# A two-layer backbone on one core: weight sums from a column of ones in the second layer's value matmul, a matmul of its own for the values' low parts, and work moved between VectorE, GpSimd and ScalarE

## Chip, cores and metric

One of the cores of a Trainium2 chip runs the whole program. The metric is the device time of one execution in microseconds; before, the median of 3 runs is 1360.35 us.

## What is computed

Two layers over 1024 latent tokens (width 1024, 16 heads of 64) and 256 context tokens, then an RMS norm. The first layer is grouped-query attention over all tokens. The second, where most of the change lies, is attention in a neighbourhood of 8 x 16 grid cells plus all context tokens, with a learned bias:

```python
px = hx @ w_in                     # q, k, v, z: 4 x 1024 columns
...
s_nb = jnp.einsum('bqhd,bqkhd->bhqk', qr, kw).astype(jnp.float32) * ATTN_SCALE + bias
s_cx = jnp.einsum('bqhd,bshd->bhqs', qr, kc).astype(jnp.float32) * ATTN_SCALE
p = jax.nn.softmax(jnp.concatenate([s_nb, s_cx], axis=-1), axis=-1)
return (einsum(p[..., :n_nb], vw) + einsum(p[..., n_nb:], vc))
...
yx = (o * jax.nn.silu(z)) @ w_out
```

## The kernel before

Everything is float32 in value, but the matmuls take float16: each operand is split into a high part and a low part (what is left after rounding), and a product takes three matmuls, high by high, high by low, low by high.

Between the layers, `ln_pair` (L692) normalizes the token rows in pairs of tiles, forms the sums and differences that the block products below need (L704 to L707, halves of 512 columns of the two tiles), splits them (L689 on ScalarE, L690 on VectorE) and sends them through transposing DMAs (L701, L712) into `hx`. Four such pairs (t = 0, 2, 4, 6) stand among the last output products of the first layer (`a_out`, L1332). TensorE's first product of the second layer, `pwq0a`, reads what the last pair leaves.

The second layer goes by pairs of heads, u = 0 to 7. For each u:

- `b_load` (L1418) loads a float32 block of the input weights, `st`, forms four sums of its blocks on GpSimd into `tt` (L1429 to L1432), and splits both into float16 (L1434 on ScalarE, L1435 on VectorE). Two kinds and four row blocks make 8 loads a pair of heads, 64 in all. `BLK` (L1438) says which slot of the weights each of the seven block products takes.
- `b_qk` and `b_vz` (L1481, L1534) make queries, keys, values and gates by `winograd` (L1440), a scheme of seven block products instead of eight, whose sums VectorE forms from PSUM (L1457 to L1478). `put` (L1490) writes queries: the high part by ScalarE (L1499), the low part by VectorE (L1500), and a second copy of the high part into the other half of the partitions (L1501). `put_v` (L1538) writes the values' high and low parts side by side, 128 columns per head, into `v1_`.
- `b_att` (L1581) takes for each head i and each of 8 query tiles t the near key tiles (two or three) and the two context tiles. Scores come from two matmuls (L1593, L1594), bias and maximum from VectorE (L1613, L1620 to L1623), and ScalarE computes the exponentials four times: into the float16 high part `bph` (L1631, L1632), and in float32 in place (L1633, L1634) with an accumulator output that gives the sum of the weights. `p_split` (L1122) takes the low part: every fourth call (`BEV`) is one operation on VectorE (L1127), the others are two halves on GpSimd (L1130). One transposing DMA (L1637) turns both parts, and four tiles later (`BLAG`) the value matmuls follow: the transposed weights are the stationary operand, loaded anew for each matmul. The high part meets all 128 columns of the values (L1642), the low part the high 64 (L1644). `fin` (L1650) adds the two halves of the result (ScalarE's copy L1657, VectorE's L1658), and multiplies by the reciprocal of the sums (L1653 to L1655, L1659) and by the gate (L1660). It runs 32 times.

The first layer's values already have the layout that the change brings: 64 high columns, a column of ones (scaled), 64 low columns, three matmuls a key tile in `pv_mm` (L1132), and `o_evict` (L1111) at the end.

The program is written in the order that `timeline` gives to the generators. A planner in the kernel then sets each engine's order anew: it lists the instructions, schedules them with its own table of costs, and five times again with due times taken from the last schedule, keeping the shortest. So a change of one operation moves others on all engines. All DMAs of the second layer stand in SyncE's queue.

## Time and profile before

| | |
|---|---|
| median of 3 runs | 1360.35 us (1357.03 to 1361.37) |
| profiled execution | 1362.21 us, its span 1360.3 us |
| mean granted TensorE clock | 0.991 |
| TensorE, VectorE, ScalarE, GpSimd busy | 1309.5, 1129.6, 976.2, 909.9 us |

The span divides into the first layer (to about 700 us), its last output products with the normalization for the second (to about 775 us), the first pair's projections (to about 850 us), attention of one pair beside projections of the next (850 to 1250 us), and the last output product with the rest. A row of a listing gives line, engine, operation, out<-in, shapes and count, then the busy time and the mean ns of one, then the idle time of the engine ahead of it and what ended that. A row of the timeline starts with start and length in us. PEld is TensorE's weight load, which overlaps its matmuls.

### The profile page before, as it was taken

Reading aid. Unit: us, or ns where it says so; the run is one execution under the profiler, and the core shown is the slowest. Engines: PE = TensorE matmul, PEld = TensorE weight load, DVE = VectorE, ACT = ScalarE, POOL = GpSimd, SP = SyncE. Lnnn points to the kernel's source line nnn. Section 1 sums busy time; section 2 is a strip of 40 time slices with the busy share of each in tenths; the row PEclk is TensorE's granted clock in tenths of the full one; section 3 lists DMA queues with packets and bytes.
Section 4 is the critical chain, followed back from the end, with each engine's and each line's share of the span. In section 5 each row is a group of like instructions: output and inputs, shape, how many; then the busy total and the mean of one; then the engine's idle time right before and its main releaser. Section 6 shows DMA issues by size and latency. Waiting matters only on the chain.

```text
span 1360.3 us, 37879 instructions
## 1 busy us (share of the span) xinstructions
PE 1309.5 (96%) x14492; PEld 923.2 (68%) x14492; DVE 1129.6 (83%) x2603; ACT 976.2 (72%) x2325; POOL 909.9 (67%) x1251
## 2 busy tenths in 40 slices
PE   8999999999999999999999899999999999999994
PEld 4467777777777777776654357868677686876551
DVE  5898687978898787769448898899999999999668
ACT  4654889888888777788733355897978889787443
POOL 2323778777777767788775566586676778755565
PEclk9999999999999999999999999999999999999997
DMA  9634566787874222245237953587677768679953
GB/s 368 186 114 114 118 125 144 153 153 146 141 142 104 66 77 60 57 118 139 79 109 175 219 109 90 115 151 146 121 142 151 150 130 173 126 165 257 262 113 124
DMA packets 390350, 191.58 MB, mean 141 GB/s; under 512 B 349776, under 2 KB 355088, under 8 KB 390168
## 3 DMA queue, kind: packets, MB, share of 16 engines
q1 hardware_dynamic: 389592, 189.13, 61.6%
q8 instruction: 113, 1.85, 0.6%
q14 instruction: 69, 0.57, 0.1%
q10 hardware_dynamic: 576, 0.03, 0.0%
HBM read 91.03 MB, written 15.75 MB: 78 GB/s over the span
## 4 chain that ended last, share of the span: by engine, by line
PE 49%; DVE 24%; ACT 11%; issue 6%; DMA 5%; POOL 4%; DVEq 0%; POOLq 0%; SPq 0%; ACTq 0%
PE pa L1034 12%; PE pob L1747 5%; PE st L1260 3%; PE st L1261 3%; DVE wb L1435 3%; PE pm L1068 3%; PE poa L1353 2%; PE pv L1137 2%; PE pv L1136 2%; PE pv L1138 2%; DVE bpf L1613 2%; DVE bk L1504 2%; DVE bmx L1620 2%; ACT bpf L1633 1%; ACT bph L1631 1%
## 5 line engine op out<-in xcount | busy, mean ns | idle before, releaser
L1130 POOL TENSOR_TENSOR pl<-pf,ph 128x256 f16<-128x256 f32 x400 | 274.8, 712 | 83.3 <-ACT pf L1247 59.0
L1130 POOL TENSOR_TENSOR bph<-bpf,bph 128x256 f16<-128x256 f32 (+1 forms) x192 | 167.5, 889 | 119.0 <-ACT bpf L1633 98.7
L1034 PE MATMUL pa<-wa,x 128*128 128x256 f16 x1536 | 219.3, 272 | 1.0 <-DVE q L822 1.0
L1245 ACT ACTIVATE ph<-st 128x512 f16<-128x512 f32 x240 | 143.2, 602 | 56.4 <-PE st L1261 55.1
L1560 PEld LDWEIGHTS <-hx 128*128 128x128 f16 x2688 | 156.7, 98 | 11.7 <-issue 4.9
L1034 PEld LDWEIGHTS <-x 128*128 128x128 f16 x1536 | 139.7, 97 | 33.2 <-DVE q L822 1.3
L1247 ACT ACTIVATE pf<-st 128x512 f32<-128x512 f32 x240 | 143.2, 603 | 1.9 <-POOL pl L1130 1.2
L1069 DVE TENSOR_REDUCE mxp<-pm 128x1 f32<-128x512 f32 x192 | 127.5, 683 | 16.2 <-PE pm L1068 15.1
L1137 PE MATMUL pv<-v,ph 128*128 128x64 f16 x960 | 122.5, 195 | 0.0
L1136 PE MATMUL pv<-v,ph 128*128 128x65 f16 x960 | 122.1, 193 | 0.0
L1138 PE MATMUL pv<-v,pl 128*128 128x65 f16 x960 | 121.5, 192 | 0.4 <-POOL pl L1130 0.4
L1512 PEld LDWEIGHTS <-wb 128*128 128x128 f16 x672 | 63.5, 99 | 81.2 <-issue 10.9
L1130 POOL TENSOR_TENSOR qpp<-qpf,qpp 128x256 f16<-128x256 f32 (+1 forms) x158 | 94.2, 621 | 33.8 <-ACT qpf L1203 25.7
L1631 ACT ACTIVATE bph<-bpf,bnx 128x384 f16<-128x384 f32 (+1 forms) x128 | 69.9, 581 | 55.7 <-DVE bnx L1623 35.6
L1136 PEld LDWEIGHTS <-ph 128*128 128x128 f16 x960 | 90.7, 96 | 23.2 <-DVE og L1118 1.7
L1137 PEld LDWEIGHTS <-ph 128*128 128x128 f16 x960 | 90.3, 97 | 14.4 <-issue 0.4
L1138 PEld LDWEIGHTS <-pl 128*128 128x128 f16 x960 | 91.1, 99 | 9.4 <-POOL pl L1130 1.1
L1260 PE MATMUL st<-q,k 128*128 128x512 f16 x240 | 90.9, 379 | 1.9 <-ACT pf L1247 1.2
L1261 PE MATMUL st<-q,k 65*128 65x512 f16 x240 | 91.2, 381 | 0.0
L1353 PE MATMUL poa<-woa,oa 128*128 128x512 f16 x384 | 89.7, 379 | 0.0
L1747 PE MATMUL pob<-wob,obf 128*128 128x512 f16 x336 | 79.9, 379 | 0.2 <-DVE tmb L1751 0.2
L1633 ACT ACTIVATE bpf<-bpf,bnx 128x384 f32<-128x384 f32 (+1 forms) x128 | 74.4, 581 | 0.2
(486 smaller groups left out, 4045.6 us busy)
## 6 DMA issues: line engine op xcount, KB each, us to landing
wg<-in_w_mb SPq DMA_DIRECT2D x32, 512.0 KB
wsb<-in_b_wp SPq DMA_DIRECT2D x64, 256.0 KB
wm<-in_w_m SPq DMA_DIRECT2D x16, 512.0 KB
wsa<-in_a_wq SPq DMA_DIRECT2D x32, 256.0 KB
xstage<-in_x SPq DMA_DIRECT2D x8, 512.0 KB
wsoa<-in_a_w_out SPq DMA_DIRECT2D x16, 256.0 KB
x<-in_x SPq DMA_DIRECT2D x8, 512.0 KB
x_d<-x SPq DMA_DIRECT2D x8, 512.0 KB
```

What stands on the lines that cost most here:

```text
L1034: T.matmul(ps[:, :, i, :], hA(a, kt, t), wt[w][:, kt, :], start=n == 0, stop=n == 3 * KT - 1)
L1069: V.tensor_reduce(mxs[i][:, t, ch:ch + 1], pm, axis=AX.X, op=ALU.max)
L1130: G.tensor_tensor(lo[:, c], p32[:, c], hi[:, c], op=ALU.subtract)
L1136: T.matmul(pv[:, t, :], hi[:, c], v[:, 0:65], start=first and t == 0, stop=False)
L1137: T.matmul(pv[:, t, 0:HD], hi[:, c], v[:, 65:129], start=False, stop=False)
L1138: T.matmul(pv[:, t, :], lo[:, c], v[:, 0:65], start=False, stop=last and t == n - 1)
L1245: S.activation(ph, st, AF.Exp)
L1247: S.activation(p32, st, AF.Exp)
L1260: T.matmul(so, k1[:, g, kc], q1[:, :, i, :], start=True, stop=False)
L1261: T.matmul(so, k2[0:65, g, kc], q2[0:65, :, i, :], start=False, stop=True)
L1560: T.matmul(ps[:, t * P:(t + 1) * P], hx[a][:, t, blk, kt], wt[j][:, s_, w, kt], start=first and t == 0 and m == 0, stop=last and t == 3 an ...
L1747: T.matmul(ps, ob[kt][:, t, a], wout["b"][hf][b][:, kt, :], start=n == 0, stop=n == 3 * len(kts) - 1)
```

## The change

- `BEV` goes from 4 to 8: every eighth split goes to VectorE.
- `ln_pair`: the sum (L704) and the second difference (L706) go from GpSimd to VectorE, as one operation each with a factor -1; the first difference (L705) goes from VectorE to GpSimd. Signs come out the same.
- `b_load`: the blocks are stored in another order, so that two of the four sums become one operation with a broadcast operand; four operations on GpSimd become three. `BLK` and the context products follow the new order of slots.
- `b_qk`: the second copy of the query's high part is computed by ScalarE from the float32 source, where VectorE copied the float16 result.
- Values of the second layer get the first layer's layout: 64 high columns, a column of ones, 64 low columns, with a memset of that column on GpSimd per pair of heads. The value product of a key tile takes three matmuls (65, 64, 65 columns) where it took two (128, 64), and the sum of the weights comes out as column 64. The two float32 exponentials lose their accumulator outputs, and `fin` becomes `o_evict`: a reciprocal and two products.

```diff
-BEV, BLAG = 4, 4
+BEV, BLAG = 8, 4
...
-        G.tensor_tensor(b2, b1, b2, op=ALU.add)
-        V.tensor_tensor(b1, a1, b1, op=ALU.subtract)
-        G.tensor_tensor(a1, b2, a1, op=ALU.subtract)
+        V.scalar_tensor_tensor(b2, b1, -1.0, b2, op0=ALU.mult, op1=ALU.subtract)
+        G.tensor_tensor(b1, a1, b1, op=ALU.subtract)
+        V.scalar_tensor_tensor(a1, b2, -1.0, a1, op0=ALU.mult, op1=ALU.subtract)
         V.tensor_tensor(a2, a2, a1, op=ALU.subtract)
...
-            b12, b11, b21, b22 = (st[:, j] for j in range(4))
-            t1, t2, t3, t4 = (tt[:, j] for j in range(4))
-            G.tensor_tensor(t1, b12, b11, op=ALU.subtract)
-            G.tensor_tensor(t2, b22, t1, op=ALU.subtract)
-            G.tensor_tensor(t3, b22, b12, op=ALU.subtract)
+            b12, b11, b22, b21 = (st[:, j] for j in range(4))
+            t1, t3, t2, t4 = (tt[:, j] for j in range(4))
+            G.tensor_tensor(tt[:, 0:2], st[:, 1:3], b12.unsqueeze(1).broadcast_to([P, 2, P]), op=ALU.subtract)
+            G.tensor_tensor(t2, b22, t1, op=ALU.add)
             G.tensor_tensor(t4, b21, t2, op=ALU.subtract)
...
-        v1_ = bq.tile([P, NT, 2, P], F16, name=f"bv1{u}", tag="v1")
+        v1_ = bq.tile([P, NT, 2, 130], F16, name=f"bv1{u}", tag="v1")
+        G.memset(v1_[:, :, :, HD:HD + 1], 2.0 * WS * WS)
...
-                    V.tensor_copy(ov[0][oth, i, ts], ov[0][own, i, ts])
+                    S.activation(ov[0][oth, i, ts], src, AF.Copy, scale=sc)
...
-            V.tensor_tensor(v1_[:, ts, :, HD:P], vv, v1_[:, ts, :, 0:HD], op=ALU.subtract)
+            V.tensor_tensor(v1_[:, ts, :, 65:129], vv, v1_[:, ts, :, 0:HD], op=ALU.subtract)
...
-                        S.activation(pf[:, 0:n], pf[:, 0:n], AF.Exp, bias=m, accum_out=sums[:, t % 4, 0:1])
-                        S.activation(pf[:, n:n + 2], cx_, AF.Exp, bias=m, accum_out=sums[:, t % 4, 1:2])
+                        S.activation(pf[:, 0:n], pf[:, 0:n], AF.Exp, bias=m)
+                        S.activation(pf[:, n:n + 2], cx_, AF.Exp, bias=m)
...
-                                T.matmul(pv[:, t % 4, :], pht[:, x_], v1_[:, kt, i, :], start=t % 4 == 0 and x_ == 0,
-                                         stop=False)
-                                T.matmul(pv[:, t % 4, 0:HD], plt[:, x_], v1_[:, kt, i, 0:HD], start=False,
+                                T.matmul(pv[:, t % 4, 0:65], pht[:, x_], v1_[:, kt, i, 0:65],
+                                         start=t % 4 == 0 and x_ == 0, stop=False)
+                                T.matmul(pv[:, t % 4, 0:HD], pht[:, x_], v1_[:, kt, i, 65:129], start=False, stop=False)
+                                T.matmul(pv[:, t % 4, 0:65], plt[:, x_], v1_[:, kt, i, 0:65], start=False,
...
-                    V.tensor_reduce(sm, sums, axis=AX.X, op=ALU.add)
-                    V.tensor_scalar_mul(sm, sm, 2.0 * WS * WS)
-                    V.reciprocal(sm, sm)
-                    oc = bl.tile([P, 4, HD], F32, name="boc" + nm, tag="boc", bufs=1)
-                    S.copy(oc, pv[:, :, HD:P])
-                    V.tensor_tensor(oc, pv[:, :, 0:HD], oc, op=ALU.add)
-                    V.tensor_tensor(oc, oc, sm.unsqueeze(2).broadcast_to([P, 4, HD]), op=ALU.mult)
-                    V.tensor_tensor(og[:, :, i * HD:(i + 1) * HD], oc, sz[:, hf * 4:hf * 4 + 4, i * HD:(i + 1) * HD],
-                                    op=ALU.mult)
+                    o_evict(bl, pv, og, 4, sz, hf * 4, i, f"b{u}{i}{hf}")
```

Line numbers behind L1424 are smaller after the change: L1435 becomes L1434, L1613 L1612, L1658 to L1660 the L1114 to L1118 of `o_evict`.

How this moves instructions is shown at three places. The first is TensorE at the first value product of the second layer (u = 0, behind the context scores `bsc` of a query tile; `bpht` are the transposed weights, `bv` the values, `bpv` the result). Before, one key tile:

```order
L1594 LDWEIGHTS bq_13809
L1594 MATMUL bsc_15362<-bk_14431,bq_13809 128x256
L1642 LDWEIGHTS bpht_15198
L1642 MATMUL bpv_15146<-bv_14432,bpht_15198 128x128
L1644 LDWEIGHTS bpht_15198
L1644 MATMUL bpv_15146<-bv_14432,bpht_15198 128x64
```

After, at the same place:

```order
L1594 LDWEIGHTS bq_13809
L1594 MATMUL bsc_15348<-bk_14427,bq_13809 128x256
L1641 LDWEIGHTS bpht_15187
L1641 MATMUL bpv_15135<-bv_14428,bpht_15187 128x65
L1643 LDWEIGHTS bpht_15187
L1643 MATMUL bpv_15135<-bv_14428,bpht_15187 128x64
L1644 LDWEIGHTS bpht_15187
L1644 MATMUL bpv_15135<-bv_14428,bpht_15187 128x65
```

One pair of weight load and matmul has come in per key tile, and the place in the queue is the same.

The second is VectorE at the last pair of normalized tiles (`x_14161` and `x_14056` are the two tiles, `hrb6a` the rows split first, `hrb6s` those of the sums). Before:

```order
L690 TENSOR_TENSOR hrb6a_14253<-x_14161,hrb6a_14252 128x512
L678 TENSOR_TENSOR x_14056<-x_14056,lrow_13844 128x512
L690 TENSOR_TENSOR hrb6a_14253<-x_14056,hrb6a_14252 128x512
L705 TENSOR_TENSOR x_14161<-x_14056,x_14161 128x512
L690 TENSOR_TENSOR hrb6a_14253<-x_14056,hrb6a_14252 128x512
L1435 TENSOR_SCALAR wb_14356<-wsb_14358,wb_14356 128x3x128
L707 TENSOR_TENSOR x_14056<-x_14056 128x512
L690 TENSOR_TENSOR hrb6s_14287<-x_14161,hrb6s_14286 128x512
```

After:

```order
L690 TENSOR_TENSOR hrb6a_14253<-x_14056,hrb6a_14252 128x512
L690 TENSOR_TENSOR hrb6a_14253<-x_14161,hrb6a_14252 128x512
L690 TENSOR_TENSOR hrb6a_14253<-x_14056,hrb6a_14252 128x512
L704 TENSOR_SCALAR x_14161<-x_14161 128x512
L1357 TENSOR_TENSOR tm_14249<-poa_14224,gt_14220 128x512
L1434 TENSOR_SCALAR wb_14356<-wsb_14358,wb_14356 128x3x128
L706 TENSOR_SCALAR x_14056<-x_14161,x_14056 128x512
L690 TENSOR_TENSOR hrb6s_14287<-x_14161,hrb6s_14286 128x512
L707 TENSOR_TENSOR x_14056<-x_14056 128x512
```

L705, which needs GpSimd's L704, has left VectorE; it stood ahead of the third `hrb6a` piece. L704 and L706 stand there now, behind all three pieces.

The third is VectorE in the first pair's attention, where the second pair's queries are written (`c22q`, `c21q`, `c12q` are sums of block products, `bq` the queries, `boc` and `bse` tiles of `fin`, `orsb` its reciprocals in `o_evict`). Before:

```order
L1470 TENSOR_TENSOR c22q_15443<-w2q_15398,pwq1c 128x512
L1474 TENSOR_TENSOR c21q_15502<-e1q_15245,pwq1b 128x512
L1500 TENSOR_SCALAR bq_13810<-c22q_15443,bq_15154 64x4x128
L1501 COPY bq_15154<-bq_15154 64x4x128
L1500 TENSOR_SCALAR bq_13810<-c22q_15443,bq_15154 64x4x128
L1613 ISA bpf_15559,bmx_15558<-bsn_15560,tb_14631 128x384
L1613 ISA bmx_15558 128x1
L1478 TENSOR_TENSOR c12q_15537<-w1q_15300,pwq1c 128x512
L1127 TENSOR_TENSOR bph_15514<-bpf_15463,bph_15514 128x640
```

After:

```order
L1500 TENSOR_SCALAR bq_13810<-c22q_15442,bq_15142 64x4x128
L1621 TENSOR_REDUCE bnx_15479<-bmx_15453 128x2
L1500 TENSOR_SCALAR bq_13810<-c22q_15442,bq_15142 64x4x128
L1622 TENSOR_SCALAR bnx_15479<-bnx_15479 128x2
L1114 RECIPROCAL orsb_15526<-bpv_15135 128x4
L1434 TENSOR_SCALAR wb_15670<-wtb_15672,wb_15670 128x4x128
L1116 TENSOR_TENSOR bpv_15135<-bpv_15135,orsb_15526 128x4x64
L1477 TENSOR_TENSOR c12q_15536<-w1q_15287,pwq1c 128x512
L1118 TENSOR_TENSOR bog_15134<-bpv_15135,bsz_14430 128x4x64
```

The copies L1501 are gone from between the low parts, and the whole end of a half head stands as three operations that read PSUM.

More of the change, by code (lines that the diff above doesn't have):

```diff
@@ L1436, in b_load @@
             yield 1.0
-    BLK = {1: (0, 0, 0), 2: (1, 0, 1), 3: (4, 0, 2), 4: (2, 1, 3), 5: (6, 1, 0), 6: (3, 1, 1), 7: (5, 1, 2)}
+    BLK = {1: (0, 0, 0), 2: (1, 0, 2), 3: (4, 0, 1), 4: (2, 1, 3), 5: (6, 1, 0), 6: (3, 1, 2), 7: (5, 1, 1)}
     def winograd(nm, mm, put):
@@ L1521, in ctx_k @@
                 for a, b in ((0, 0), (0, 1), (1, 0)):
-                    T.matmul(ps[:, 0:NC * P].rearrange("p (t q) -> p t q", q=P), wt[0][:, kt // 4, a, kt % 4],
+                    T.matmul(ps[:, 0:NC * P].rearrange("p (t q) -> p t q", q=P), wt[0][:, kt // 4 * 2, a, kt % 4],
                              hc[b][:, :, kt], start=m == 0, stop=m == 3 * KT - 1)
@@ L1571, in ctx_v @@
                     for a, w in ((0, 0), (0, 1), (1, 0)):
-                        T.matmul(ps[:, t * P:(t + 1) * P], hc[a][:, t, kt], wt[0][:, kt // 4, w, kt % 4],
+                        T.matmul(ps[:, t * P:(t + 1) * P], hc[a][:, t, kt], wt[0][:, kt // 4 * 2, w, kt % 4],
                                  start=t == 0 and m == 0, stop=t == NC - 1 and m == 3 * KT - 1)
@@ L1600, in b_att @@
                 pv = psum.tile([P, 4, P], F32, name=f"bpv{u}{i}{hf}", tag="pv", bufs=2)
-                sums = bl.tile([P, 4, 2], F32, name=f"bsm{u}{i}{hf}", tag="sums", bufs=2)
                 for t0 in (hf * 4, hf * 4 + 2):
@@ L1648, in b_att, with fin @@
                         yield 625
-                def fin(pv=pv, sums=sums, og=og, i=i, hf=hf):
-                    nm = f"{u}{i}{hf}"
-                    sm = bl.tile([P, 4], F32, name="bse" + nm, tag="bse", bufs=2)
-                    V.tensor_reduce(sm, sums, axis=AX.X, op=ALU.add)
-                    V.tensor_scalar_mul(sm, sm, 2.0 * WS * WS)
-                    V.reciprocal(sm, sm)
-                    oc = bl.tile([P, 4, HD], F32, name="boc" + nm, tag="boc", bufs=1)
-                    S.copy(oc, pv[:, :, HD:P])
-                    V.tensor_tensor(oc, pv[:, :, 0:HD], oc, op=ALU.add)
-                    V.tensor_tensor(oc, oc, sm.unsqueeze(2).broadcast_to([P, 4, HD]), op=ALU.mult)
-                    V.tensor_tensor(og[:, :, i * HD:(i + 1) * HD], oc, sz[:, hf * 4:hf * 4 + 4, i * HD:(i + 1) * HD],
-                                    op=ALU.mult)
+                def fin(pv=pv, og=og, i=i, hf=hf):
+                    o_evict(bl, pv, og, 4, sz, hf * 4, i, f"b{u}{i}{hf}")
                     if i == 1:
@@ L1824 @@
         "a_w_out": i["a_w_out"][0],
-        "b_wp": np.stack([np.stack([wb[h, :, :, r] for h, r in ((0, r2), (0, r1), (1, r1), (1, r2))], 2)
+        "b_wp": np.stack([np.stack([wb[h, :, :, r] for h, r in ((0, r2), (0, r1), (1, r2), (1, r1))], 2)
                           for r1, r2 in ((1, 0), (2, 3))]).transpose(4, 0, 1, 2, 3, 5),
```

## The prediction

> **What bounds the kernel now.** I read the page's first part, then the windows by stage, and then what the stops of TensorE ended on.
>
> The first part of the page (engine, busy time, share of the span, instructions):
>
> ```profile
> PE 1309.5 (96%) x14492; PEld 923.2 (68%) x14492; DVE 1129.6 (83%) x2603; ACT 976.2 (72%) x2325; POOL 909.9 (67%) x1251
> ```
>
> TensorE is nearly full. The change lies in the second layer, so I cut that layer into stages (busy time of PE, PEld, DVE, ACT, POOL in each stretch, then granted clock, DMA share, GB/s):
>
> ```profile
> 780.00:785.00 5.00, 4.43 (x11) 1.43 (x10) 5.00 (x8) 1.01 (x3) 3.96 (x5) 0.50 1.10 221
> 785.00:790.00 5.00, 4.85 (x15) 1.88 (x15) 4.74 (x8) 3.34 (x7) 5.00 (x6) 0.62 0.33 83
> ...
> 850.00:1250.00 400.00, 389.70 (x4853) 304.64 (x4851) 380.37 (x890) 335.73 (x917) 283.30 (x392) 1.00 0.75 148
> 1250.00:1324.00 74.00, 73.98 (x493) 39.17 (x492) 47.72 (x97) 34.91 (x100) 41.03 (x39) 1.00 0.84 215
> ```
>
> From 850 to 1250 us two engines are nearly full at once: TensorE 389.7 and VectorE 380.4 of 400. From 1250 to 1324 TensorE stops for nothing. What TensorE stopped for in the 400 us (total, times, longest):
>
> ```profile
> PE pwv7c L1560 <- DVE bv L1542: 1.3, 1, 1.3
> PE pwq6b L1512 <- DVE w2q L1465: 1.2, 1, 1.2
> PE pwq2b L1512 <- DVE bk L1504: 1.0, 1, 1.0
> PE bpv L1642 <- DMA bpht<-bph: 1.0, 1, 1.0
> PE pwq5a L1512 <- ACT e1q L1453: 0.9, 1, 0.9
> ```
>
> Three of the five longest end on VectorE, which with 95% busy is often late with what TensorE needs next. The visible stops are 400 - 389.7 = 10.3 us. A matmul's bar also covers its drain: the first row below lasts 220 ns, but the next two rows, four keys apart, are 0.34 us apart, 85 ns a key, whose two matmuls have 128 and 64 columns. So a stop hides up to about 0.16 us more. For some 16 stops that is 2.6 us, and I take 13 us as what can be won here.
>
> ```profile
> L1642 PE MATMUL bpv<-bv,bpht x608: 217/220/229, 845.9 to 1324.3; 128*128 128x128 f16 x152
> ...
> 900.78 0.22 PE L1642 MATMUL bpv<-bv,bpht 128*128 128x128 f16 x1
> 901.12 0.81 PE L1512 MATMUL pwq2b<-hx,wb 128*128 128x512 f16 x3
> ```
>
> **The price on TensorE.** Each of the 608 key blocks now takes three load and matmul pairs (65, 64, 65 columns) instead of two. The first layer runs just this triple. Eleven matmuls lie between these two rows:
>
> ```profile
> 499.82 0.19 PE L1136 MATMUL pv<-v,ph 128*128 128x65 f16 x1
> ...
> 500.16 0.38 PE L1034 MATMUL pa<-wa,x 128*128 128x256 f16 x2
> ```
>
> That is 0.34 us / 11 = 31 ns each, 93 ns a key, and so (93 - 85) x 608 = **+4.9 us** on the fullest engine. The ends are 0 and, if each pair cost what a 128-column one does (85 less 28 for the short one is about 57 ns, so 171 ns a key), +52 us. I take the first layer's value, since shapes and order are the same.
>
> **What leaves the other engines.** Rows are line, shapes, count, busy time, mean ns:
>
> ```profile
> L1659 DVE TENSOR_TENSOR boc<-boc,bse 128x256 f32<-128x256 f32 x32 | 18.2, 570 | 0.1
> L1660 DVE TENSOR_TENSOR bog<-boc,bsz 128x256 f32<-128x256 f32 x32 | 18.0, 563 | 0.1
> L1501 DVE COPY bq<-bq 64x512 f16<-64x512 f16 x32 | 17.0, 542 | 0.7
> ...
> L1654 DVE TENSOR_SCALAR bse<-bse 128x4 f32<-128x4 f32 x32 | 13.4, 420 | 0.1
> L1658 DVE TENSOR_TENSOR boc<-bpv,boc 128x256 f32<-128x256 f32 x32 | 13.3, 415 | 1.3 <-ACT boc L1657 1.2
> L1657 ACT COPY boc<-bpv 128x256 f32<-128x256 f32 x32 | 11.8, 369 | 7.8 <-PE bpv L1644 7.6
> ```
>
> ```profile
> L1116 DVE TENSOR_TENSOR pv<-pv,ors 128x256 f32<-128x256 f32 x24 | 10.2, 427 | 0.3
> L1118 DVE TENSOR_TENSOR og<-pv,sz 128x256 f32<-128x256 f32 x24 | 10.0, 418 | 0.2
> ```
>
> The end of a half head loses four VectorE operations (570 + 563 + 420 + 415 = 1968 ns; the small reduce is left out and the reciprocal stays) and gains o_evict's two (845 ns). That is 1123 ns x 32 = 35.9 us off VectorE, and 11.8 us off ScalarE. The query copies take 17.0 us off VectorE and put 32 activations of 64x512 on ScalarE, at the 626 ns of the like row below +20.0 us.
>
> ```profile
> L1130 POOL TENSOR_TENSOR bph<-bpf,bph 128x256 f16<-128x256 f32 (+1 forms) x192 | 167.5, 889 | 119.0 <-ACT bpf L1633 98.7 <-ACT bpf L1634 10.8 <-issue 8.7
> L1429 POOL TENSOR_TENSOR wtb<-wsb 128x128 f32<-128x128 f32 x64 | 39.3, 614 | 26.1 <-DMA wsb<-in_b_wp 15.1 <-DVE wb L1435 5.2 <-DVE c22v L1470 1.5
> L1432 POOL TENSOR_TENSOR wtb<-wsb,wtb 128x128 f32<-128x128 f32 x64 | 38.1, 596 | 0.0
> L1127 DVE TENSOR_TENSOR bph<-bpf,bph 128x640 f16<-128x640 f32 (+1 forms) x32 | 31.8, 992 | 2.0 <-ACT bpf L1634 1.7
> L1634 ACT ACTIVATION_READ_ACCUMULATOR bpf<-bsc,bnx 128x1 f32 x128 | 25.8, 201 | 0.0
> L1633 ACT ACTIVATION_READ_ACCUMULATOR bpf<-bpf,bnx 128x1 f32 x128 | 24.7, 193 | 0.0
> L1499 ACT ACTIVATE bq<-c22q 64x512 f16<-64x512 f32 x16 | 10.0, 626 | 0.2
> ```
>
> With BEV 8, half of VectorE's 32 splits go: -15.9 us there, and 32 more halves on GpSimd at 889 ns, +28.4 us. GpSimd's weight sums lose one of four operations, but one becomes twice as wide. Its price lies between one narrow operation (614 ns) and two (1228 ns); I take the 889 ns of the nearest wide row. Then 64 x (614 + 596 - 889) = 20.5 us leave GpSimd (38.5 at best, none at worst), and it ends some 8 us busier, plus eight tiny memsets. It had 283 of 400 us, and work before it to wait for (119 us idle ahead of its splits alone), so I cost that at nothing for TensorE. If that cover is gone, a split's end, its transpose and the value matmul come later by 16 x (2 x 889 - 992) = 12.6 us in all at most. ScalarE loses 50.5 us of accumulator reads. Sums: VectorE -35.9 - 17.0 - 15.9 = **-69 us**, ScalarE 20.0 - 11.8 - 50.5 = **-42 us**, nearly all from 845 us on. Seven eighths of VectorE's, 60 us, lie in the 400 us stage: 380 becomes 320, 80% instead of 95%. The end of what TensorE waited for there then comes early, and the next late ones are ScalarE and the transposes, 0.9 and 1.0 us in the rows above. I take **9 of the 13 us** as won; the ends are 0 and 13.
>
> **The turn between the layers.** TensorE's rows (idle before in brackets), then VectorE's:
>
> ```profile
> 753.78 20.88 PE L1353 MATMUL poa<-woa,oc 128*128 128x512 f16 x96
> 778.28 0.39 PE L1512 MATMUL pwq0a<-hx,wb 128*128 128x512 f16 x1 [3.62 <-DMA hx<-hrb6a]
> 779.58 4.85 PE L1512 MATMUL pwq0a<-hx,wb 128*128 128x512 f16 x11 [0.90 <-DMA hx<-hrb6a]
> ```
>
> ```profile
> 756.71 2.63 DVE L705 TENSOR_TENSOR x<-x,x 128x512 f32<-128x512 f32 x1 [1.24 <-POOL x L704]
> 773.28 0.69 DVE L705 TENSOR_TENSOR x<-x,x 128x512 f32<-128x512 f32 x1 [1.16 <-POOL x L704]
> ```
>
> TensorE stands for 3.62 + 0.90 us until the last pair of rows is normalized and transposed. VectorE's stream ahead of that waits twice for GpSimd's L704 and once takes 2.63 us for what takes 0.69 us elsewhere. In the new order L704 and L706 are VectorE's own and all three hrb6a pieces stand ahead of L704. The pair ahead gains 1.24 us of wait and about 1.9 us of the slow operation, and pays 0.7 us for one operation more: 2.5 us. Another 1.2 us is the last pair's wait, ahead of its third piece. I take **3.5 us**, of up to 4.5 us of stop, and -1.4 us at the other end (the added operation twice, no wait saved). One more thing depends on it: behind the stop the clock is granted at 0.50 and 0.62 in the two windows, which costs up to 5 x 0.50 + 5 x 0.38 = 4.4 us. I leave that out, since VectorE is busy 5.00 and 4.74 of 5 us in just these windows and would be the next to be late.
>
> [...]
>
> **The tail.** PE's transposes of the last head waited for its end:
>
> ```profile
> 1329.89 0.63 PE L1150 MATMUL pob<-idf,bog 128*128 128x128 f32 x4 [0.38 <-DVE bog L1660]
> ```
>
> With 1.1 us less ahead of it I take **1 us** (0 to 2).
>
> **Sum.** +4.9 - 9 - 3.5 - 1 = -8.6 us. The profiled execution took 1362.21 us (span 1360.3), so 1353.6; it stands 1.86 us over the median of the three runs shown, and against that median the forecast is **1352 us** (1360.35 - 8.6 = 1351.75). With 6 to 12 us won in the stage and 2 to 4.5 us at the turn its own range is 1348 to 1356.
>
> **Rivals.**
> 1. *The clock stays whole.* If the stop of 3.62 us shrinks far enough, the half-clock stretch goes too: 4.4 us more, 1347 us. For it speaks that 3.5 us off the stop leave next to nothing; against it, VectorE full in the same windows.
> 2. *The waits form again.* The plan of every engine is made anew, and ScalarE (336 of 400 us) and the transposes then end the stops. If a third of the 13 us is won (4) and 1.5 us at the turn, the sum is +4.9 - 4 - 1.5 = -0.6: 1360 us. For it: two of the five longest waits aren't VectorE's. Against it: ScalarE loses 42 us too, and the transposes stay as many as they were.
> 3. *Slower: the third weight load isn't hidden.* Place: the value matmuls between 850 and 1324 us. All winnings, 13.5 us, are eaten at 13.5 / 608 = 22 ns more a key, 107 instead of 85; from 114 ns it is slower by over 0.3%. At three full pairs, 171 ns, it is +52 - 13.5 = +38.5: 1399 us. For it: PEld is busy 305 of 400 us in this stage. Against it: the first layer's 93 ns.
>
> [...]
>
> **How the numbers follow.** Forecast 0.57, first rival 0.17, second 0.17, third 0.09. A measurement of this kernel tells about 0.3%, 4 us, from no change. Forecast and first rival are faster by more than that, but for 0.01 at the forecast's edge; the second is within it, but for 0.01 slower. So faster 0.73, same 0.17, slower 0.10. For 8 in 10 the range goes from 1343 (the first rival with all 13 us won) to 1359, which takes in the forecast's ends and the better half of the second rival; the third is left out.
>
> **What would show it.** The value triples at about 93 ns a key; VectorE near 320 of 400 us in the middle stage, and TensorE's visible stops there down from 10.3 to some 3 us; L705 on GpSimd with no VectorE wait of over 1 us ahead of it; the first pwq0a matmul 2 to 4 us closer behind the last poa; a granted clock of 0.50 or 1.00 behind that stop, which decides the first rival. The prediction is wrong if the triples take over 107 ns a key, or if the stops stay near 10 us with ScalarE, GpSimd or the transposes as what ends them.

## The result and the profile after

| | before | after |
|---|---|---|
| median of 20 runs | 1360.12 us (1356.3 to 1362.81) | 1355.87 us (1354.15 to 1357.94) |
| profiled execution, its span | 1362.21 us, 1360.3 us | 1355.27 us, 1353.5 us |

The changed kernel is faster by 4.25 us: ratio 0.997, 95% interval 0.9963 to 0.9977. That is half of the 8.6 us forecast; the median lies 3.9 us above the 1352 forecast, at the slow end of the forecast's own range (1348 to 1356). The two profiled executions lie 6.94 us apart, since that of before is 2.1 us above its median and that of after 0.6 us below.

The page's first part for the changed kernel (engine, busy time, share, instructions):

```profile
PE 1309.8 (97%) x15100; PEld 927.4 (69%) x15100; DVE 1067.0 (79%) x2463; ACT 961.4 (71%) x2069; POOL 905.4 (67%) x1223
```

VectorE lost 62.6 us (forecast 69), GpSimd 4.5 (forecast 8 more), ScalarE only 14.8 (forecast 42). The stages of the second layer, columns as in the prediction:

```profile
780.00:785.00 5.00, 5.00 (x25) 2.17 (x23) 3.69 (x6) 1.59 (x4) 5.00 (x4) 1.00 0.48 124
785.00:790.00 5.00, 4.48 (x23) 2.04 (x21) 4.88 (x7) 2.06 (x5) 5.00 (x6) 1.00 0.20 54
790.00:795.00 5.00, 1.27 (x8) 0.51 (x7) 5.00 (x8) 2.81 (x5) 2.55 (x4) 0.82 0.43 103
795.00:800.00 5.00, 3.58 (x11) 1.45 (x11) 4.94 (x10) 3.46 (x7) 1.83 (x3) 0.50 0.72 161
...
850.00:1250.00 400.00, 396.44 (x5405) 311.34 (x5403) 344.30 (x788) 327.51 (x704) 288.01 (x381) 1.00 0.79 157
```

In the middle stage TensorE's visible stops went from 10.3 to 3.6 us, as forecast. What they ended on (total, times, longest):

```profile
PE pwv6c L1560 <- DVE bv L1542: 0.9, 1, 0.9
PE bpv L1641 <- DMA bpht<-bph: 0.9, 3, 0.4
PE bsn L1593 <- DVE bmx L1612: 0.5, 1, 0.5
PE pwq7b L1512 <- DVE bk L1504: 0.5, 1, 0.5
```

The half clock at 780 to 790 is gone. But in the two windows behind, TensorE now stands for 5.2 of 10 us. TensorE's timeline shows why (idle before a row in brackets):

```profile
775.32 0.38 PE L1512 MATMUL pwq0a<-hx,wb 128*128 128x512 f16 x1
775.93 1.02 PE L1512 MATMUL pwq0a<-hx,wb 128*128 128x512 f16 x4 [0.23 <-DMA hx<-hrb6a]
...
791.62 0.22 PE L1560 MATMUL pwv0c<-wb,hx 128*128 128x128 f16 x1 [1.00 <-ACT wb L1433]
...
796.30 0.48 PE L1560 MATMUL pwv0c<-wb,hx 128*128 128x128 f16 x3 [4.03 <-DVE wb L1434]
796.90 4.27 PE L1512 MATMUL pwq0b<-hx,wb 128*128 128x512 f16 x12
```

The first pwq0a follows the first layer's last product without a stop, 0.2 us after the last one's start, where before the change it waited 3.62 us and came 4.0 us after. A stop of 4.03 us, in which the clock falls to 0.50, now stands 18 us later, at a product (pwv0c) that the planner put between those of pwq0b; the kernel before had it there too, without such a wait. VectorE's rows ahead of the weights that it waits for:

```profile
788.06 1.93 DVE L677 SCALAR_TENSOR_TENSOR x<-x,rs_ln,lrow 128x512 f32<-128x512 f32 x2
789.92 1.54 DVE L678 TENSOR_TENSOR x<-x,lrow 128x512 f32<-128x512 f32 x2
...
794.37 1.28 DVE L678 TENSOR_TENSOR x<-x,lrow 128x512 f32<-128x512 f32 x2
795.57 0.68 DVE L1434 SCALAR_TENSOR_TENSOR wb<-wtb,wb 128x512 f16<-128x512 f32 x1
```

From 788 to 795.6 VectorE normalizes the two context tiles and begins to split them; the split of the weights (L1434) comes behind them.

To see where the time went I measure from the first layer's last product (start of the last poa). The code ahead of it, which the change touches only in the normalization's sums, ends at 771.8 to 780.5 us in the kernels below. Each row gives the least, median and greatest duration in ns, then the first and the last start; I take the last start of poa and the first of pwq1a and pwq7a:

```profile
L1353 PE MATMUL poa<-woa,oc x96: 378/379/380, 754.6 to 775.1; 128*128 128x512 f16 x96
```

```profile
L1512 PE MATMUL pwq1a<-hx,wb x24: 379/379/380, 831.0 to 839.6; 128*128 128x512 f16 x24
```

```profile
L1512 PE MATMUL pwq7a<-hx,wb x24: 378/380/380, 1177.9 to 1188.0; 128*128 128x512 f16 x24
```

| us, profiled executions | before | after | difference |
|---|---|---|---|
| to the last poa | 774.3 | 775.1 | +0.8 |
| to the first pwq1a (turn, first pair) | 58.8 | 55.9 | -2.9 |
| to the first pwq7a (pairs 1 to 6) | 352.2 | 346.9 | -5.3 |
| to the end | 175.0 | 175.6 | +0.6 |
| last poa to the end | 586.0 | 578.4 | -7.6 |

### The profile page after: what moved, and what is told of

Same layout as the page of the kernel before. It is cut to its first block, busy times and chain, and to the rows that moved or that the text cites. A ratio compares the mean times of both kernels' runs of the same rounds, so it can differ in the third digit from the quotient of the medians.

```text
span 1353.5 us, 38686 instructions
## 1 busy us (share of the span) xinstructions
PE 1309.8 (97%) x15100; PEld 927.4 (69%) x15100; DVE 1067.0 (79%) x2463; ACT 961.4 (71%) x2069; POOL 905.4 (67%) x1223
## 5 line engine op out<-in xcount | busy, mean ns | idle before, releaser
L1130 POOL TENSOR_TENSOR pl<-pf,ph 128x256 f16<-128x256 f32 x400 | 275.0, 711 | 83.7 <-ACT pf L1247 58.3
L1130 POOL TENSOR_TENSOR bph<-bpf,bph 128x256 f16<-128x256 f32 (+1 forms) x224 | 180.0, 829 | 98.6 <-ACT bpf L1632 66.6
L1245 ACT ACTIVATE ph<-st 128x512 f16<-128x512 f32 x240 | 143.2, 602 | 56.3 <-PE st L1261 55.0
L1429 POOL TENSOR_TENSOR wtb<-wsb 128x256 f32<-128x256 f32 x64 | 59.3, 928 | 38.5 <-DMA wsb<-in_b_wp 14.9
```

What stands on the lines that cost most here:

```text
L1130: G.tensor_tensor(lo[:, c], p32[:, c], hi[:, c], op=ALU.subtract)
L1245: S.activation(ph, st, AF.Exp)
```

## The experiments

My theory after the result: the value part's relief wins TensorE's stops in the middle stage, and the price per key is as forecast; the turn's winnings are mostly handed back at pwv0c. Rivals: the 4 us are the luck of one plan, since the planner sets every engine's order anew; or ScalarE's relief, not VectorE's, won the stops.

### The same programs in other orders

The planner's slack for due times is changed, in both kernels; every instruction stays, and the planner makes another order, called a plan below. The edit for 320:

```diff
-        plan.refine(5, 100.0, 300.0)
+        plan.refine(5, 100.0, 320.0)
```

> The changed kernel with every instruction the same and another order: the planner's slack for due times is 320 instead of 300. It measures what a plan by itself is worth. Theory (the 4 us come from the work that was moved): within 2 us of 1356. Rival (the 4 us lie within what one plan differs from another): 3 us or more away from 1356, on either side.

> The kernel before with every instruction the same and another order: the planner's slack for due times is 280 instead of 300. It measures how far one plan of the kernel before lies from another. Theory (the change is worth its 4 to 8 us in whatever order): between the last product of the first layer and the end the kernel before takes 584 to 590 us in each of its plans, and the changed kernel 577 to 586; the time as a whole lies 1356 to 1366 us. Rival (the 4 us are the luck of one plan): some plan of the kernel before reaches 580 us in that stretch, or 1356 as a whole.

> The kernel before with every instruction the same and another order: the planner's slack is 320, the value at which the changed kernel took 1365.0 us. Theory (the change is worth its 4 to 8 us in whatever order): 1369 to 1373 us, that is 4 to 8 us slower than the changed kernel with the same slack. Rival (the plan decides): 1365 us or less.

> The changed kernel with every instruction the same and another order: the planner's slack is 280. Theory (the change is worth its 4 to 8 us in whatever order): 4 to 8 us faster than the kernel before with the same slack. Rival (the plan decides): no faster than it.

| slack | before, median | after, median | last poa to the end, before | after |
|---|---|---|---|---|
| 280 | 1366.12 | 1360.17 | 590.6 | 583.3 |
| 300 | 1360.12 | 1355.87 | 586.0 | 578.4 |
| 320 | 1369.21 | 1365.01 | 592.3 | 585.5 |

Against the kernel before the ratios are 1.0048 (1.0032 to 1.0065) and 1.0001 (0.9989 to 1.0012) at 280, 1.0067 (1.0048 to 1.0085) and 1.0036 (1.0022 to 1.005) at 320. A plan alone moves a kernel by 4 to 9 us, as much as the change does or more: within 2 us, as I expected of the changed kernel at 320, was wrong, and its rival right with 9. The kernel before also came out slower than I expected of its other plans (590.6 and 592.3 us in that stretch, against 584 to 590). But at each slack the changed kernel is ahead, by 5.9, 4.2 and 4.2 us in the medians and by 7.3, 7.6 and 6.8 us from the last poa to the end in the profiles. No plan of the kernel before reaches 1356 us, and in that stretch each plan after (578.4 to 585.5) is shorter than each plan before (586.0 to 592.3). In the three plans tried, the gain is the change's, not one plan's luck. The middle stage of the changed kernel at 280 and 320, then of the kernel before at 280 and 320:

```profile
850.00:1250.00 400.00, 395.51 (x5400) 310.91 (x5399) 346.69 (x784) 328.56 (x705) 286.51 (x382) 1.00 0.79 155
```

```profile
850.00:1250.00 400.00, 392.96 (x5383) 308.92 (x5382) 336.94 (x773) 328.51 (x703) 284.23 (x378) 1.00 0.79 152
```

```profile
850.00:1250.00 400.00, 387.48 (x4821) 302.48 (x4819) 383.77 (x885) 333.39 (x909) 284.05 (x388) 1.00 0.75 148
```

```profile
850.00:1250.00 400.00, 385.26 (x4807) 301.63 (x4807) 381.45 (x874) 331.53 (x901) 278.50 (x388) 1.00 0.74 145
```

Visible stops fall from 12.5 to 4.5 us and from 14.7 to 7.0, as from 10.3 to 3.6 at 300: 6.7 to 8.0 us in each plan. From the first pwq1a to the first pwq7a the changed kernel is 5.7 us shorter at 280 and 5.3 at 320, as at 300. The turn isn't so steady: from the last poa to the first pwq1a it is 59.3 and 59.6 us at 280, 59.0 and 57.4 at 320, so +0.3, -2.9 and -1.6 us in the three plans.

### One part undone, order left to the planner

The value part as before (values, two matmuls, accumulators, the end of a half head):

```diff
...
-                                T.matmul(pv[:, t % 4, 0:65], pht[:, x_], v1_[:, kt, i, 0:65],
-                                         start=t % 4 == 0 and x_ == 0, stop=False)
-                                T.matmul(pv[:, t % 4, 0:HD], pht[:, x_], v1_[:, kt, i, 65:129], start=False, stop=False)
-                                T.matmul(pv[:, t % 4, 0:65], plt[:, x_], v1_[:, kt, i, 0:65], start=False,
+                                T.matmul(pv[:, t % 4, :], pht[:, x_], v1_[:, kt, i, :], start=t % 4 == 0 and x_ == 0,
+                                         stop=False)
+                                T.matmul(pv[:, t % 4, 0:HD], plt[:, x_], v1_[:, kt, i, 0:HD], start=False,
...
```

> The changed kernel, but the second layer's values, value matmuls, accumulators and the end of a half head as before. Theory (the value part's relief and its price nearly cancel): TensorE gets 4.6 us back (608 keys at 87 instead of 94 ns), VectorE gets some 36 us and ScalarE some 62 us more to do, and visible stops in the middle stage rise from 3.6 us to 6 to 8; the time is within 2 us of the changed kernel's 1356, and the value part by itself is worth about nothing. Rival A (the value part carries the gain): stops back near 10 us, 1358 to 1361. Rival B (the value part only costs, the other moves carry the gain): stops stay at 4 us and the time falls to 1351.

The median is 1359.79 us (ratio to before 0.9995, 0.9982 to 1.0007), 3.9 over the changed kernel, 581.1 us from the last poa to the end. In the middle stage:

```profile
850.00:1250.00 400.00, 389.92 (x4858) 305.33 (x4857) 370.21 (x854) 354.34 (x945) 288.90 (x374) 1.00 0.78 154
```

The stops are 10.1 us, as many as before the change: rival A, in both of its numbers. With the query copies and splits moved but the value part left out, VectorE falls from 380 to 370 and ScalarE rises from 336 to 354, and nothing is won in the stage. The 3.9 us are no more than a plan can move a kernel; the stops differ by more than in any two plans of one kernel.

The order of sums between the layers as before (in the changed kernel L704's sum and the first weight difference both have the opposite sign of before, which cancels in the products; here the sum alone is turned back, so its products are those of other numbers, while operations and sizes are the same):

```diff
-        V.scalar_tensor_tensor(b2, b1, -1.0, b2, op0=ALU.mult, op1=ALU.subtract)
-        G.tensor_tensor(b1, a1, b1, op=ALU.subtract)
-        V.scalar_tensor_tensor(a1, b2, -1.0, a1, op0=ALU.mult, op1=ALU.subtract)
+        G.tensor_tensor(b2, b1, b2, op=ALU.add)
+        V.tensor_tensor(b1, a1, b1, op=ALU.subtract)
+        G.tensor_tensor(a1, b2, a1, op=ALU.subtract)
```

> The changed kernel with the sum and second difference between the layers back on GpSimd and the first difference on VectorE. Theory (the turn's 3 us are won there and then handed back at pwv0c): the stop at the first pwq0a comes back with 3 to 4 us and the half clock stands behind it again, the stop of 4.0 us at pwv0c goes, and the time is within 2 us of 1356. Rival (the turn's gain was kept): 3 to 5 us slower than the changed kernel, 1359 to 1361, about the kernel before.

1363.79 us (ratio 1.0034, 1.0021 to 1.0046). Its last poa starts at 777.8 us, and the first pwq1a follows after 58.3, 2.4 us more than in the changed kernel. The stops at pwv0c shrink to 1.30 and 1.82 us, and one of 2.24 us comes back at pwq0a; but it stands behind eleven of its matmuls, ends on VectorE's weight split (L1434) and has no half clock behind it (1.00 from 780 to 795). So the theory is right in part only, and the whole is 8 us slower, which fits neither; it can't be told from a plan's effect.

The fifth product of the first pair's values in the later pairs' place:

```diff
-        first = nm[1:] == "0"
+        first = nm == "q0"
```

> The changed kernel, but for the values of the first pair of heads the fifth block product is written in the place that it has for the later pairs, so that the planner puts no pwv0c matmul between those of pwq0b. Theory (the turn's winnings went to the wait of 4.0 + 1.0 us at pwv0c and to the half clock behind it): no stop over 1.5 us between 775 and 830, the clock at 1.00 there, the first pwq1a 4 to 7 us earlier than 831.0, and the whole 3 to 7 us faster, 1349 to 1353. Rival A (TensorE waits as long for whatever stands there, since the weights or VectorE are late): the stop reappears at pwq0b or pwv0a, time within 1.5 us of 1356. Rival B (what is won at the first pair is given back by 1235, because a later wait decides): pwq1a earlier, end the same.

1365.14 us (ratio 1.0031, 1.0018 to 1.0045). No pwv0c stands among pwq0b any more, and the clock is whole (1.00) from 765 to 810, but TensorE waits there all the same:

```profile
797.28 2.75 PE L1512 MATMUL pwq0b<-hx,wb 128*128 128x512 f16 x12 [3.08 <-DVE w1q L1456]
801.47 2.75 PE L1512 MATMUL pwq0b<-hx,wb 128*128 128x512 f16 x12 [1.45 <-DVE w2q L1464]
```

The first pwq1a comes 56.7 us after the last poa (changed kernel 55.9). Rival A holds for the stop, which comes back at pwq0b: not the place of pwv0c but VectorE's lateness makes it. Rival A's time doesn't: the whole is 9 us slower than 1356, 5.4 of them ahead of the last poa, which is a plan's effect. So a run with less for VectorE there was made, below.

### One cost changed at exactly the same order

Since a plan alone moves the time by 4 us and more, these five runs change what instructions cost and tell the planner the old cost, so that each engine runs its instructions in the changed kernel's own order. Their medians are set against the changed kernel's 1355.87; the kernel before had medians of 1359.45 to 1360.73 beside the different runs, so a difference of 1 us says nothing.

The third value matmul with 2 columns:

```diff
-            cols = self.elems(outs[0])
+            cols = HD if self.elems(outs[0]) == 2 and outs[0].bass_ap.tensor.name[:3] == "bpv" else self.elems(outs[0])
...
-                                T.matmul(pv[:, t % 4, 0:HD], pht[:, x_], v1_[:, kt, i, 65:129], start=False, stop=False)
+                                T.matmul(pv[:, t % 4, 0:2], pht[:, x_], v1_[:, kt, i, 65:67], start=False, stop=False)
```

> The changed kernel in exactly its own order of instructions on every engine (the planner is told the old width), but the third value matmul, high weights by low values, has 2 columns instead of 64; it leaves out nearly all of the values' low parts. It asks whether TensorE sets the pace where the price was paid. Theory (TensorE-bound from 850 to 1324 us): whatever a key gets shorter, times 608, comes off the end, but for up to 2 us of stops that come back; at 75 instead of 94 ns a key that is 11.5 us, 1344 to 1348. Rival A (another engine sets the pace): the key is shorter, and the end moves by less than a third of that. Rival B (the weight load, not the columns, sets a pair's time): the key stays above 90 ns and nothing moves.

1354.14 us (ratio 0.9947, 0.9934 to 0.996), 1.7 us less than the changed kernel; 577.1 from the last poa. Five keys in a row, of the changed kernel:

```profile
848.58 0.19 PE L1641 MATMUL bpv<-bv,bpht 128*128 128x65 f16 x1
848.61 0.20 PE L1643 MATMUL bpv<-bv,bpht 128*128 128x64 f16 x1
848.64 0.19 PE L1644 MATMUL bpv<-bv,bpht 128*128 128x65 f16 x1
...
849.04 0.59 PE L1512 MATMUL pwq1c<-hx,wb 128*128 128x512 f16 x2
```

and of this one:

```profile
1004.76 0.19 PE L1641 MATMUL bpv<-bv,bpht 128*128 128x65 f16 x1
1004.79 0.17 PE L1643 MATMUL bpv<-bv,bpht 128*128 128x2 f16 x1
1004.82 0.19 PE L1644 MATMUL bpv<-bv,bpht 128*128 128x65 f16 x1
...
1005.20 2.75 PE L1512 MATMUL pwq4a<-hx,wb 128*128 128x512 f16 x12
```

That is 0.46 / 5 = 92 ns a key against 0.44 / 5 = 88. With 2 columns in one of the three pairs they take 29 ns each on the mean, against 31, so rival B is nearly right in its number: the columns hardly count at this size. That the weight load is what sets a pair's time is not shown. The 4 ns that were saved, times 608, are 2.4 us, and 1.7 came off the median. That agrees with a TensorE that sets the pace, but this run moved it too little to show it.

The accumulator outputs back, into a tile that nothing reads:

```diff
-                        S.activation(pf[:, 0:n], pf[:, 0:n], AF.Exp, bias=m)
-                        S.activation(pf[:, n:n + 2], cx_, AF.Exp, bias=m)
+                        S.activation(pf[:, 0:n], pf[:, 0:n], AF.Exp, bias=m, accum_out=sums[:, 32 * u + 16 * i + 2 * t:][:, 0:1])
+                        S.activation(pf[:, n:n + 2], cx_, AF.Exp, bias=m, accum_out=sums[:, 32 * u + 16 * i + 2 * t:][:, 1:2])
...
```

> The changed kernel in exactly its own order of instructions, but the two float32 exponentials have an accumulator output again (written to a tile that nothing reads), so that ScalarE has its 256 accumulator reads of about 197 ns back, 50 us. It asks what that part of the relief was worth. Theory (VectorE's relief won the stops, ScalarE's little of it): ScalarE 328 to some 370 of 400 us, visible stops up from 3.6 by 0 to 2 us, the whole within 2 us of the changed kernel's 1356. Rival (ScalarE's relief carried the gain): stops back at 8 us or more, 1360 or slower.

1367.61 us (ratio 1.005, 1.0037 to 1.0064), 11.7 us slower than the changed kernel. The theory fell: ScalarE's relief is worth that much at this order. The middle stage and the stops:

```profile
850.00:1250.00 400.00, 387.63 (x5318) 304.92 (x5314) 332.20 (x764) 341.04 (x909) 277.18 (x372) 1.00 0.78 149
```

```profile
PE bpv L1641 <- DMA bpht<-bph: 2.7, 5, 1.0
PE pwv6c L1560 <- DVE bv L1542: 1.4, 1, 1.4
PE pwv7c L1560 <- DVE bnx L1621: 1.4, 1, 1.4
```

12.4 us of stops, more than before the change, and two of the three longest end on VectorE. Only ScalarE's instructions differ, so VectorE's lateness comes from there. VectorE's row of the narrower weight splits, of the changed kernel and then of this run, agrees: its wait for ScalarE's half (last number) grows from 10.7 to 16.1 us.

```profile
L1434 DVE SCALAR_TENSOR_TENSOR wb<-wsb,wb 128x384 f16<-128x384 f32 x64 | 47.6, 749 | 10.9 <-ACT wb L1433 10.7
```

```profile
L1434 DVE SCALAR_TENSOR_TENSOR wb<-wsb,wb 128x384 f16<-128x384 f32 x64 | 45.2, 712 | 16.5 <-ACT wb L1433 16.1
```

The page gives ScalarE 984.9 us, 23.5 more, not 50. ScalarE's rows in this run show why:

```profile
1004.30 0.18 ACT L1632 ACTIVATION_READ_ACCUMULATOR bpf<-bpf,bnx 128x1 f32 x1
1004.39 0.45 ACT L1633 ACTIVATE bpf<-bsc,bnx 128x256 f32<-128x256 f32 x1
1004.75 0.19 ACT L1633 ACTIVATION_READ_ACCUMULATOR bpf<-bsc,bnx 128x1 f32 x1
1004.84 0.36 ACT L1541 CAST bv<-pvc 128x256 f16<-128x256 f32 x1
```

A read lasts 0.18 to 0.19 us, but the next instruction starts 0.09 us after it: rows overlap, and a read costs 23.5 / 256 = 92 ns.

The reciprocal at the end of a half head over more elements (520, then 180), read from PSUM. The edit for 180:

```diff
...
-        V.reciprocal(rs[:, 0:n], pv[:, 0:n, 64])
+        V.reciprocal(rs if w else rs[:, 0:n], pv[:, 0:n, 20:65] if w else pv[:, 0:n, 64]); rs = rs[:, :, 44] if w else rs
```

> The changed kernel in exactly its own order of instructions, but the reciprocal at the end of each of the 32 half heads runs over 520 elements from PSUM instead of 4; the values used are the same. VectorE gets some 0.4 to 0.6 us x 32 = 13 to 19 us back of the 62.6 that it lost. Theory (VectorE's relief won the stops, and what is left of slack is small): visible stops of the middle stage up from 3.6 by 1 to 4 us, the whole 1 to 4 us slower than the changed kernel, 1357 to 1360. Rival (VectorE has slack at 86% busy): within 1 us of 1356.

1441.8 us (ratio 1.0592, 1.0575 to 1.061), 86 us slower: the operation was not 0.4 to 0.6 us longer but 3.2.

```profile
L1114 DVE RECIPROCAL orsb<-bpv 128x520 f32<-128x520 f32 x32 | 108.7, 3398 | 12.7 <-PE bpv L1644 12.7
```

That put 32 x 3.2 = 103 us of rows on VectorE instead of 13 to 19, far more than was taken off, so the run doesn't answer the question. The next does:

> The changed kernel in exactly its own order of instructions, but the reciprocal at the end of each half head runs over 180 elements from PSUM instead of 4; the values used are the same. The run with 520 elements took 3397 ns a time instead of 172, 6.25 ns an element, so this one should take some 1.27 us: 1.1 us x 32 = 35 us more on VectorE, as much as the value part took off it at the end of a half head. Theory (VectorE's and ScalarE's relief are both needed, and either put back at the same order brings the stops back): visible stops of the middle stage from 3.6 to 8 to 14 us, the whole 6 to 12 us slower than the changed kernel's 1356, as the 51 us of accumulators made it. Rival (only ScalarE was short): stops up by less than 3 us, the whole within 3 us of 1356.

```profile
L1114 DVE RECIPROCAL orsb<-bpv 128x180 f32<-128x180 f32 x32 | 40.7, 1273 | 10.2 <-PE bpv L1644 10.2
```

```profile
850.00:1250.00 400.00, 382.94 (x5271) 301.38 (x5269) 352.16 (x744) 315.51 (x675) 269.77 (x366) 1.00 0.74 145
```

1376.15 us (ratio 1.0118, 1.0097 to 1.0139): 35 us of rows on VectorE (30.5 of its busy time on the page) cost 20 us at the end, and the stops are 17.1 us. The direction is the theory's, the size beyond its range. So both reliefs are needed. At a fixed order either one put back costs more than the whole change brings, since the order was made for the shorter operations; what a plan made for them would win back isn't in these two figures.

Less for VectorE at the turn: the normalization of the context tiles over 32 of 512 columns.

```diff
-            c = slice(hf * 512, hf * 512 + 512)
+            c = slice(hf * 512, hf * 512 + (32 if v else 512))
```

> The changed kernel in exactly its own order of instructions, but the normalization of the two context tiles multiplies and adds only 32 of each 512 columns (it leaves the other columns unnormalized), which takes some 5 us off VectorE between 788 and 795.6 us. It asks what the stop of 4.0 us at pwv0c hangs on. Theory (VectorE's stream of context rows stands ahead of the weights that pwv0c waits for, and the turn's winnings were lost there): the stop falls below 1.5 us, the clock is 1.00 from 790 to 800, the first pwq1a comes 4 to 6 us before 831.0 and the whole is 4 to 6 us faster, 1350 to 1352. Rival A (GpSimd's weight sums or a DMA are just as late): the stop moves to another cause and the first pwq1a comes less than 2 us earlier. Rival B (a later wait decides): pwq1a earlier, the end the same.

1352.63 us (ratio 0.9938, 0.9926 to 0.995), 3.2 us less than the changed kernel. The stop shrank from 4.03 to 2.16 us, and the first pwq1a starts 52.2 us after the last poa instead of 55.9 (54.7 to 56.3 in the five executions of this order with the full context rows):

```profile
792.87 0.47 PE L1560 MATMUL pwv0c<-wb,hx 128*128 128x128 f16 x3 [2.16 <-DVE wb L1434]
793.47 4.05 PE L1512 MATMUL pwq0b<-hx,wb 128*128 128x512 f16 x12
```

So about half of the stop hangs on VectorE's stream of context rows, and 3.7 us of the turn were lost there; from the last poa to the end 2.2 of them remain (576.2). Some 1.9 of the 3.7 us are the shorter stop; another 1.7, as an estimate, the half clock, which lasts 3.4 us here where it lasted 6.8 (half of the 3.4 between them). The direction is the theory's, but none of its numbers was reached: VectorE now waits 1.16 us in between for ScalarE's L689, the stop stays above 1.5 us, and the clock is still halved around it.

The splits' new share, the weight sums in three operations and the query copy were not tried alone, since each makes a new plan.

## Why the prediction was right or wrong

- **TensorE's price** (+4.9 us): right. 92 ns a key instead of 85 is 7 x 608 = 4.3 us. The third rival (weight loads not hidden) is out: it needed 107 ns.
- **The middle stage** (-9 us): right in size, in three plans. From the first pwq1a to the first pwq7a the profile shows -5.3 us net, with most of the price in it (-5.7 and -5.3 in the other plans). The reason was half right. I put the stops down to VectorE alone, since three of the five longest ended there. Put back at a fixed order, 35 us on VectorE cost 20 us, and 23.5 us on ScalarE cost 11.7. A wait that ends on VectorE can have its cause in ScalarE.
- **VectorE near 320 us**: it came to 344. The removed operations took 61 us of rows out of the stage, as summed, but rows that follow each other overlap by up to some 0.08 us, and the busy time counts an overlap once: all rows of the stage together went from 435.5 to 388.9 us (-46.6), the busy time from 380.4 to 344.3 (-36.1). So 10.5 us were lost by adding durations. The other 14.5 are rows that took longer or came in, the weight splits above all. VectorE's rows of that stage, of before and of after (busy time, mean ns):

```profile
L1435 DVE SCALAR_TENSOR_TENSOR wb<-wtb,wb 128x512 f16<-128x512 f32 x48 | 39.5, 824 | 5.1 <-ACT wb L1434 5.0
...
L1435 DVE SCALAR_TENSOR_TENSOR wb<-wsb,wb 128x384 f16<-128x384 f32 x48 | 31.5, 662 | 0.2
```

```profile
L1434 DVE SCALAR_TENSOR_TENSOR wb<-wtb,wb 128x512 f16<-128x512 f32 x48 | 41.8, 871 | 2.2 <-ACT wb L1433 2.0
...
L1434 DVE SCALAR_TENSOR_TENSOR wb<-wsb,wb 128x384 f16<-128x384 f32 x48 | 35.7, 747 | 8.6 <-ACT wb L1433 8.5
```

  That is 6.5 us for the same 96 operations; of the rest, 4.9 us are four more splits of the output weights (L731) that now fall into the window. Why the weight splits take longer wasn't tried.
- **ScalarE's -42 us**: here too the durations were added as if they followed each other. All its rows together fell by 41.5 us (1170.3 to 1128.8), but the accumulator reads cost 92 ns each, not 197, and the busy time fell by 14.8 us.
- **GpSimd** (+8 us): it came to -4.5. The 32 more halves added some 15 us of rows, since a half now takes 829 ns on the mean of its widths where it took 889; the weight sums lost 14.7 (the merged one takes 928 ns, I took 889), and the normalization, which the sum left out, 6.5. No stop of TensorE listed above ends on GpSimd, as forecast.
- **The turn** (-3.5 us): the step that failed. The stop at the first pwq0a went, and VectorE's waits with it, but I counted the stop as won. The prediction itself named VectorE, full in just these windows, as next to be late, and used that only against the first rival. It was late: -2.9 us in the profile, with 3.7 more lost to the next stop as the run with less context work shows, and +0.3 and -1.6 in the other plans. The mean of the three plans is -1.4, a 2.1 us smaller term. With the three runs of the section on one part undone, the five plans with the normalization's new order take 55.2 to 59.6 us there (mean 57.0), the four with the old one 58.3 to 59.3 (mean 58.9): 1.9 us, by programs that differ in other ways too. Part of the spread is the half clock, which at the turn lasted from nothing to 10.2 us in these profiles, and 6.8 or 3.4 us in one and the same order.
- **The tail** (-1 us): mis-sized. The transposes no longer wait, but from the last value matmul to the end it is 35.7 us (1353.5 - 1317.8) instead of 36.0 (1360.3 - 1324.3): 0.3.
- **The sum against one execution**: from the last poa the profiles show -7.6 us, near the -8.6; the medians show 4.25. Six executions with the changed kernel's order have their last poa between 773.7 and 777.2 us, so one pair of profiles doesn't resolve the last 2 to 3 us. Where the rest of the difference lies stays open.
- **First rival**: its condition came true (clock 1.00 from 775 to 790), its gain did not, for the half clock moved to 793. The 3.62 us stop before the change had half the clock behind it (0.50 from 780 to 785). The 4.03 us stop began at 792.3, and the clock fell at 793.2 (0.79 on the mean of the first row below), 0.9 us into it. Behind the stop of 2.16 us it was halved too (rows of that run below), while stops of 3.08 us (the run with pwv0c moved) and 2.24 us (the sums as before) left it whole. So the length of one stop didn't decide, and that a stop leaves the clock whole once it has shrunk far enough, as the first rival assumes, is not shown. What does decide isn't shown either. The rows behind these figures, of the changed kernel and then of the run with less context work:

```profile
792.00:794.00 2.00, 0.27 (x2) 0.00 (x0) 2.00 (x4) 1.73 (x4) 0.63 (x1) 0.79 0.47 140
```

```profile
793.00:794.00 1.00, 0.88 (x5) 0.44 (x4) 1.00 (x2) 0.58 (x2) 0.92 (x2) 0.50 0.97 192
...
796.00:798.00 2.00, 2.00 (x10) 0.92 (x9) 2.00 (x4) 1.94 (x4) 0.00 (x0) 0.97 0.75 171
```

- **Second rival** (waits form again): not in any of the three plans.

## What to carry to other kernels

Where a planner sets the order anew, one pair of kernels measures the change and the plan together; the same pair at two more settings of the planner, or one cost changed at a fixed order, tells them apart. Beside a TensorE that is 97% busy, ask of each wait not only which engine ended it but what that engine had waited for. A stop that goes is won only if the next thing on the same late engine isn't due soon behind it (here 3.62 us went, and 4.03 us came 18 us later). And durations of rows can't be added to a busy time where rows overlap (here 46.6 us of VectorE's rows were 36.1 us of its busy time): measure from start to start.

## What was not expected of the hardware

- VectorE's reciprocal takes (3398 - 1273) / (520 - 180) = 6.25 ns an element, where a product of 256 elements from PSUM takes 424 ns in all.
- A key of three load and matmul pairs takes 92 ns with 65, 64 and 65 columns and 88 with 65, 2 and 65: 31 and 29 ns a pair on the mean of the three.
- A stop of 2.16 us was followed by half the clock, and ones of 3.62 and 4.03 us were, but ones of 2.24 and 3.08 us were not. By the granted clock in windows of 1 and 2 us, the half clock ran from 778.5 to 788.8 us in the kernel before, from 793.2 to 800.0 in the changed one and from 792.7 to 796.1 in the run with less context work: 10.2, 6.8 and 3.4 us, which are three, two and one times 3.4. In the changed kernel's order the clock from 775 to 850 us was 0.95 on the mean in three executions (the changed kernel's, the one with 2 columns, the one with the accumulators back) and 0.98 in a fourth (the reciprocal over 520 elements), as with less context work: by these means about half as much half clock, as an estimate.
